# Value products in joint batches, unbroken first products of the compression, and another block order in the first feed-forward layer

## The chip, the cores and the metric

The kernel runs on one core of one Trainium2 chip. The metric is the device time of one execution in microseconds (us). Three runs of the kernel before took 1014.2, 1014.8 and 1014.85 us; their median is 1014.8 us.

## What is computed

The reference is a small transformer of two layers on one sequence of 256 tokens, 1024 wide, all in float32. Each layer is a feed-forward step, a mixer and a second feed-forward step, each added to the running `x`:

```python
x = x + 0.5 * swiglu(rms_norm(x, ffa_norm[l]), ffa_w_gate[l], ffa_w_up[l], ffa_w_down[l])
x = x + hybrid_mixer(rms_norm(x, mix_norm[l]), w_in[l], ...)
x = x + 0.5 * swiglu(rms_norm(x, ffb_norm[l]), ffb_w_gate[l], ffb_w_up[l], ffb_w_down[l])
```

`swiglu(x) = (silu(x @ w_gate) * (x @ w_up)) @ w_down`, with a hidden width of 2816. The mixer projects to 2840 columns. Eight of its heads (64 wide) do causal attention within the one block of 256 tokens. The other eight share two key-value heads and add three branches under sigmoid gates: attention over compressed blocks, over selected blocks, and within a window. At this length the selected blocks and the window each cover all earlier tokens, so that both are plain causal attention. The compression takes 32 tokens of 64 columns (2048 numbers) per block, multiplies by `w1` (2048 x 256), applies a gelu, and multiplies by `w2` (256 x 64). Both halves of the mixer are normalised and multiplied by `w_out`.

## The kernel before

Weights come as 1 MB transfers into five `raw` buffers. ScalarE rounds each half of such a buffer to float32r (`whi`, L301), VectorE takes the rest (`wlo`, L280), and TensorE adds three products, hi x hi, lo x hi and hi x lo (`prod3`, L320 to L322). There are six buffers for each of `whi` and `wlo`; TensorE frees them.

**Feed-forward.** Gate and up are cut into column blocks of 512. A plan, one per feed-forward step, is a list of tokens: `g0`, `u0`, `g2` ... are whole products of a gate or up block with all of `x` (48 matmuls of 512 columns each), `h5` is the last, half-wide block of both. For blocks 1 and 3, gate and up together are made from seven block products instead of eight (`product`): a token such as `63` is product 6 of block 3, 12 matmuls. These products need sums of weight blocks. A sum is made in place: product 1 is a plain load, and 5, 6 and 4 each add one more block to the same `raw` buffer with an accumulating transfer from GpSimd's queue (L260), once the split of the sum before has been read out of it; 3 and 7 share a second buffer in the same way. Plain loads go through SyncE's queue (L246, L237). The plan's order is at once the order of the products on TensorE, of the splits on ScalarE and VectorE, of the plain loads, and of the accumulating transfers. `rest` recombines the seven results on VectorE: L628 and L630 after product 6, L633 after product 7 (it reads the bank into which product 4 then adds), L638 to L653 for the gated halves. For a plain block, L573 multiplies gate by up (tile `sg`), and `turn` (L548) transposes the result on TensorE.

**Mixer.** After the scores and the exponentials, `apply` scales four 128 x 128 pieces of probabilities, transposes them (L1059), copies them into one of two `pT` tiles, and multiplies each by a 64-wide slice of values (L1077). These four value products are one batch. Each of them uses 64 of the array's columns, so the profile shows them as `128*64`; two neighbours lie in different halves. The first products of the compression (`hidden`, L1237) use 32 columns each, `128*32`; they are given out in four groups of four, with a pause between the groups in which other work may be put. A mixer has 18 batches and two sets of 16 compression products.

**What sets the order.** Every engine runs its own list of instructions, written when the program is built. `Flow` keeps an estimated clock for each engine and steps a set of generators; a `yield` names the estimated time, event or buffer that a generator waits for, and the one that is due first writes its next instructions. Estimated times order the instructions; the chip waits on semaphores.

Of the kernel before, what the change touches and what calls it, by code (L numbers as in the profile page):

```python
# [33 lines left out]
RB = 0  # L34
RA = 1
BAL = 0.4
TH0 = 2.0
COLD = 5.0
WARM = 8
ARRIVE = [4.4, 5.2, 6.7, 7.4], [8.9, 9.6, 11.1, 11.8]  # L40
ARRIVE_X = [3.5, 5.9, 8.1, 10.3]
HOP = 0.3
PLANS = ("g0 u0 g2 11 u2 51 21 31 g4 61 71 13 u4 41 53 23 33 h5 63 73 43".split(),) + (
    "g0 u0 11 g2 51 21 31 u2 61 71 13 g4 41 53 23 33 u4 63 73 h5 43".split(),) * 3
AC = 0.1
DV = 0.06
# [85 lines left out]
def hybrid_kernel(ctx, tc, x_in, ffa_norm, ffa_w_gate, ffa_w_up, ffa_w_down, mix_norm, w_in,  # L132
# [3 lines left out]
    nc = tc.nc  # L136
# [10 lines left out]
    fl = Flow()  # L147
    NRAW, NW, NP = 5, 6, 5
    for tag, n in (("acc", 4), ("sb", 2), ("tb", 2), ("raw", NRAW), ("w", NW),
                   ("work", 7), ("p", NP), ("pT", 2), ("pair", 1)):  # L150
        fl.pool(tag, range(n))

    def bank(tag, bufs):
# [660 lines left out]
    def mixer(l, us, nm, nxt):  # L814
# [6 lines left out]
        def carve(w, *shape):  # L821
            n = 1
            for s in shape:
                n *= s
            o = pos[w]
            pos[w] += n
            assert pos[w] <= 5632
            ap = (b1, b2)[w][:, o:o + n]
            names = "abcde"[:len(shape)]
            if len(shape) > 1:  # L830
                ap = ap.rearrange(f"p ({' '.join(names)}) -> p {' '.join(names)}",
                                  **{c: s for c, s in zip(names, shape)})
            return ap
# [13 lines left out]
        w2v = carve(1, 2, 64)  # L847
        posT = carve(1, 2, 16)
        kbd = carve(1, 2, 16)
        h1T = carve(1, 2, 32)  # L850
        hid = carve(1, 256)
        th = carve(1, 2, 32)
        gT = {k: gall[:, o + 4 * l:o + 4 * l + 4] for k, o in (("m", 48), ("n", 56))}
        cs = carve(1, T, 8, 16)
        pTs = [carve(w, 512) for w in range(2)]
        k1 = big.tile([128, 2, 512], F32R, name="k1", tag="nhi")
        k2 = big.tile([128, 2, 512], F32R, name="k2", tag="nlo")
        qs = [big.tile([128, 4, 256], F32R, name="qs", tag=z) for z in ("ohi", "olo")]
# [158 lines left out]
        class Group:  # L1017


            def __init__(self, left, close):  # L1020
                self.left, self.close, self.o = left, close, None
                self.asked, self.open = False, Event()
                self.begun = set()

        def apply(grp, e, t, ents, pp, sums, gate, late):

            n = 128 * (t + 1)
            yield e
            f = small.tile([128, 4], F32, name="f", tag="f", bufs=8)[:, :len(ents)]
            nc.vector.tensor_scalar(f, sums, 1e-30, None, op0=OP.max)  # L1030
            nc.vector.reciprocal(f, f)
            e = fl.on("dve", 0.42)
            if gate is not None:
                yield gate[0]
                fv = f.rearrange("p (b h) -> p b h", h=2) if len(ents) == 4 else f
                nc.vector.tensor_tensor(fv, fv, gate[1], OP.mult)
                e = fl.on("dve", 0.25)
            wait, e0 = [], e
            for i in range(len(ents)):
                p = pp[:, i * n:(i + 1) * n]  # L1040
                if fl.eng["act"] + 0.2 + BAL < fl.eng["dve"]:
                    wait.append(i)
                else:
                    nc.vector.tensor_scalar(p, p, f[:, i:i + 1], None, op0=OP.mult)
                    e = max(e, fl.dve(n // 2))
            if wait:
                yield e0
                for i in wait:
                    p = pp[:, i * n:(i + 1) * n]
                    nc.scalar.activation(p, p, AF.Copy, scale=f[:, i:i + 1])  # L1050
                    e = max(e, fl.act(n))
            yield e
            for k in late:
                yield event(*k)
            yield fl.get("tb")
            ps = tbank()
            todo = [(s_, i) for s_ in range(t + 1) for i in range(len(ents))]
            for j, (s_, i) in enumerate(todo):
                nc.tensor.transpose(ps[:, j * 128:(j + 1) * 128],  # L1059
                                    pp[:, i * n + s_ * 128:i * n + (s_ + 1) * 128], ident)  # L1060
            yield fl.pe(0.109 * len(todo))
            fl.put("p")
            pi = yield fl.get("pT")
            pT = pTs[pi]
            e = copy(pT, ps, 512)
            fl.put("tb", 0, e)
            yield e
            if not grp.asked:
                grp.asked = True
                yield fl.get("acc")  # L1070
                grp.o = bank("acc", 4)
                grp.open.set(fl.clock)
            yield grp.open
            for j, (s_, i) in enumerate(todo):
                h, val = ents[i]
                u = h % 2
                nc.tensor.matmul(grp.o[u * 64:(u + 1) * 64, h // 2 * 128:(h // 2 + 1) * 128], val(s_),  # L1077
                                 pT[:, j * 128:(j + 1) * 128], start=u not in grp.begun,
                                 stop=gate is None and s_ == t, skip_group_check=True)
                grp.begun.add(u)  # L1080
            e = fl.pe(0.135 * len(todo))
            fl.put("pT", pi, e)
            grp.left -= 1
            if grp.left == 0:
                fl.spawn(grp.close(grp, e))

        def tile_p(t, ents, scores, gate, late, grp, free):

# [138 lines left out]
        def hidden(b):  # L1227
            u = us[("w1k", "w1v")[b]]
            for r in u:
                yield r.landed[3]  # L1230
            yield event("blk", b)
            yield fl.get("acc")
            pc = bank("acc", 4)
            for j in range(4):
                for c in range(4):
                    i = c * 4 + j
                    nc.tensor.matmul(pc[c * 32:(c + 1) * 32, :256], blk[:, b, i].rearrange("p g n -> p (g n)"),  # L1237
                                     u[i // 8].tile.rearrange("p (j c) -> p j c", j=8)[:, i % 8],
                                     start=j == 0, stop=j == 3)
                fl.pe(0.5)  # L1240
                yield
            for r in u:
                fl.put("raw")
            fl.spawn(finish_cmp(b, pc))

        def finish_cmp(b, pc):
            yield fl.clock + HOP
            nc.scalar.activation(hid, pc[:, :256], AF.Copy)
            e = fl.act(256)
            fl.put("acc", 0, e)  # L1250
            yield e
            yield fl.get("tb")
            ps = tbank()
            for c in range(2):
                nc.tensor.matmul(ps[:, c * 32:(c + 1) * 32], hid[:, c * 128:(c + 1) * 128], tab["quad"],
                                 start=True, stop=True)
            yield fl.pe(0.3)
            hv = ps[:, :64].rearrange("p (c m) -> p c m", c=2)
            nc.scalar.activation(th, hv, AF.Square)
            yield fl.act(64)  # L1260
            nc.vector.scalar_tensor_tensor(th, th, 1.0 / GELU_K, hv, op0=OP.add, op1=OP.mult)
            yield fl.dve(64)
            nc.scalar.activation(th, th, AF.Tanh, scale=GELU_C * GELU_K)
            yield fl.act(64)
            po = ps[:, 128:192]
            if b == 0:
                nc.vector.scalar_tensor_tensor(h1T, th, 1.0, hv, op0=OP.add, op1=OP.mult)
                yield fl.dve(64)
                for c in range(2):
                    nc.tensor.matmul(po[:, :32], w2kd[:, c].rearrange("p u d -> p (u d)"), h1T[:, c],  # L1270
                                     start=c == 0, stop=c == 1)
                yield fl.pe(0.3)
                nc.vector.tensor_tensor(kbd, po[:, :32].rearrange("p (g n) -> p g n", g=2),
                                        tab["km"][:, :, None].to_broadcast([128, 2, 16]), OP.mult)
                e = fl.dve(32)
            else:
                nc.vector.scalar_tensor_tensor(th, th, 1.0, hv, op0=OP.add, op1=OP.mult)
                fl.dve(64)
                nc.vector.tensor_copy(hrep.rearrange("p c (r m) -> p c r m", r=4),
                                      th[:, :, None, :].to_broadcast([128, 2, 4, 32]))  # L1280
                yield fl.dve(256)
                for c in range(2):
                    nc.tensor.matmul(po, hrep[:, c], w2v[:, c], start=c == 0, stop=c == 1)
                yield fl.pe(0.4)
                nc.vector.tensor_tensor(vbd, po[:, None, :].to_broadcast([128, 8, 64]),
                                        tab["vm"].rearrange("p g r -> p (g r)")[:, :, None].to_broadcast([128, 8, 64]),
                                        OP.mult)
                e = fl.dve(512)
            fl.put("tb", 0, e)
            event("cmp", b).set(e)  # L1290

        def cmp_heads(t):
# [322 lines left out]
```

## Time and profile before

| what | value |
|---|---|
| median of three runs | 1014.8 us |
| the profiled execution: its own time | 1014.25 us |
| the profiled execution: its span, first to last instruction | 1012.5 us |
| TensorE matmuls busy | 994.3 us, 98% |
| VectorE busy | 739.1 us, 73% |
| ScalarE busy | 604.1 us, 60% |
| mean granted TensorE clock | 0.995 |

The profile is one execution. Busy times of engines overlap. TensorE's matmuls are pipelined: the length of a row is the time that one is under way, and rows overlap; the pace is the distance between their starts. "Granted clock" is the share of full speed that TensorE gets. The chain that ended last starts from the last instruction and goes back, at each step to what released it; its lengths add up without overlap.

### The profile page before, as it was taken

How to read it: one execution, taken by the hardware profiler on the slowest of the kernel's cores; microseconds unless marked ns; L12 is line 12 of the kernel's file. 1: busy time of each engine (PE TensorE's matmuls, PEld its weight loads, DVE VectorE, ACT ScalarE, POOL GpSimd, SP SyncE). 2: the span in 40 equal slices, each digit the busy share in tenths (PEclk: the TensorE clock that was granted, in tenths of full speed). 3: DMA queues.
4: the chain of work that ended last, by engine and by line, in shares of the span. 5: the costliest groups of instructions: out<-in, count | busy, mean ns of one | idle time of the engine just before them, and what ended most of it. 6: DMA issues, size and time to landing. Idle time of an engine off the chain costs nothing.

```text
span 1012.5 us, 14210 instructions
## 1 busy us (share of the span) xinstructions
PE 994.3 (98%) x5270; PEld 826.1 (82%) x5270; DVE 739.1 (73%) x1383; ACT 604.1 (60%) x1041; POOL 53.5 (5%) x61
## 2 busy tenths in 40 slices
PE   9999989999999999999999999999999999999996
PEld 7888768899877888888888888888978778888885
DVE  6988574588787978784488778447888789688544
ACT  7666543559666766653367566336695766665431
POOL 1011100100000011100001110001000001110000
PEclk9999989999999999999999999999999999999999
DMA  9999966363833599975649998553645238999611
GB/s 336 280 242 265 249 209 207 96 208 92 309 103 122 155 245 303 252 282 177 207 132 227 288 274 265 198 177 115 208 167 209 84 125 218 281 260 303 235 55 41
DMA packets 100981, 207.62 MB, mean 205 GB/s; under 512 B 3784, under 2 KB 23376, under 8 KB 100912
## 3 DMA queue, kind: packets, MB, share of 16 engines
q1 hardware_dynamic: 83072, 171.65, 48.9%
q0 software_dynamic: 17536, 34.54, 19.2%
q8 instruction: 41, 0.67, 0.3%
q10 hardware_dynamic: 304, 0.53, 0.1%
q14 instruction: 28, 0.23, 0.1%
HBM read 205.66 MB, written 1.05 MB: 204 GB/s over the span
## 4 chain that ended last, share of the span: by engine, by line
PE 90%; DMA 4%; DVE 3%; ACT 2%; issue 1%; DVEq 0%; POOL 0%; ACTq 0%; POOLq 0%
PE acc L320 18%; PE acc L321 18%; PE acc L322 18%; PE sb L322 6%; PE sb L320 6%; PE sb L321 6%; DMA raw<-in_ffb_w_up_dram 3%; PE acc L337 2%; PE acc L338 2%; PE acc L339 2%; PE acc L1077 2%; PE tb L548 2%; PE tb L1059 2%; DVE wlo L280 1%; DMA raw<-in_ffa_w_gate_dram 1%
## 5 line engine op out<-in xcount | busy, mean ns | idle before, releaser
L280 DVE TENSOR_TENSOR wlo<-raw,whi 128x1024 fp32r<-128x1024 f32 (+2 forms) x404 | 450.2, 1136 | 173.5 <-ACT whi L301 172.6
L301 ACT ACTIVATE whi<-raw 128x1024 fp32r<-128x1024 f32 (+2 forms) x404 | 388.7, 990 | 254.2 <-PE acc L322 107.4
L320 PE MATMUL acc<-whi,xhi 128*128 128x512 f32 (+1 forms) x336 | 133.1, 396 | 5.7 <-DVE p L633 5.7
L320 PE MATMUL acc<-whi,hhi 128*128 128x512 f32 x352 | 138.4, 393 | 0.0
L322 PE MATMUL acc<-whi,hlo 128*128 128x512 f32 x352 | 137.2, 390 | 0.0
L321 PE MATMUL acc<-wlo,hhi 128*128 128x512 f32 x352 | 137.0, 389 | 0.0
L321 PE MATMUL acc<-wlo,xhi 128*128 128x512 f32 (+1 forms) x336 | 128.9, 383 | 0.0
L322 PE MATMUL acc<-whi,xlo 128*128 128x512 f32 (+1 forms) x336 | 128.5, 382 | 0.0
L320 PE MATMUL sb<-whi,xhi 128*128 128x512 f32 x304 | 119.2, 392 | 0.0
L322 PE MATMUL sb<-whi,xlo 128*128 128x512 f32 x304 | 118.4, 390 | 0.0
L321 PE MATMUL sb<-wlo,xhi 128*128 128x512 f32 x304 | 118.3, 389 | 0.0
L320 PEld LDWEIGHTS acc<-whi,xhi 128*128 128x128 f32 x336 | 63.7, 189 | 17.2 <-ACT whi L301 6.1
L322 PEld LDWEIGHTS acc<-whi,hlo 128*128 128x128 f32 x352 | 66.1, 188 | 14.0
L321 PEld LDWEIGHTS acc<-wlo,hhi 128*128 128x128 f32 x352 | 66.1, 188 | 13.5
L320 PEld LDWEIGHTS acc<-whi,hhi 128*128 128x128 f32 x352 | 66.1, 188 | 13.2
L322 PEld LDWEIGHTS acc<-whi,xlo 128*128 128x128 f32 x336 | 63.6, 189 | 12.3
L321 PEld LDWEIGHTS acc<-wlo,xhi 128*128 128x128 f32 x336 | 63.7, 190 | 10.7 <-DVE wlo L280 0.2
L322 PEld LDWEIGHTS sb<-whi,xlo 128*128 128x128 f32 x304 | 57.0, 188 | 12.0
L321 PEld LDWEIGHTS sb<-wlo,xhi 128*128 128x128 f32 x304 | 57.1, 188 | 11.7
L320 PEld LDWEIGHTS sb<-whi,xhi 128*128 128x128 f32 x304 | 57.1, 188 | 11.6
L337 PE MATMUL acc<-xhi,whi 128*128 128x256 f32 x192 | 56.4, 294 | 0.0
L338 PE MATMUL acc<-xlo,whi 128*128 128x256 f32 x192 | 54.2, 282 | 0.0
(221 smaller groups left out, 1425.3 us busy)
## 6 DMA issues: line engine op xcount, KB each, us to landing
raw<-in_ffa_w_down_dram SPq DMA_DIRECT2D x22, 1024.0 KB, 5.1
raw<-in_ffb_w_down_dram SPq DMA_DIRECT2D x22, 1024.0 KB, 5.0
raw<-in_w_in_dram SPq DMA_DIRECT2D x20, 1024.0 KB, 5.1
raw<-in_ffb_w_gate_dram SPq DMA_DIRECT2D x20, 1024.0 KB, 5.3
raw<-in_ffa_w_gate_dram SPq DMA_DIRECT2D x18, 1024.0 KB, 7.5
raw<-in_ffa_w_up_dram SPq DMA_DIRECT2D x16, 1024.0 KB, 6.9
raw<-in_ffb_w_up_dram SPq DMA_DIRECT2D x16, 1024.0 KB, 7.0
raw<-in_ffa_w_up_dram POOLq DMA_DIRECT2D x12, 1024.0 KB, 9.1
```

The costliest lines, as they stand in the source:

```text
L280: nc.vector.tensor_tensor(view(u, lo, i, True), source(u, i), view(u, hi.bitcast(F32), i, True), OP.subtract)
L301: nc.scalar.activation(view(u, u.halves[-1][0], i, True), source(u, i), AF.Copy)
L320: nc.tensor.matmul(ps, xh, wh, start=first, stop=False, skip_group_check=True)
L321: nc.tensor.matmul(ps, xh, wl, start=False, stop=False, skip_group_check=True)
L322: nc.tensor.matmul(ps, xl, wh, start=False, stop=last, skip_group_check=True)
L337: nc.tensor.matmul(ps, wh, xs[0][:, k], start=first and j == 0, stop=False, skip_group_check=True)
L338: nc.tensor.matmul(ps, wh, xs[1][:, k], start=False, stop=False, skip_group_check=True)
L339: nc.tensor.matmul(ps, wl, xs[0][:, k], start=False, stop=last, skip_group_check=True)
L548: nc.tensor.transpose(ps[:, j * 128:(j + 1) * 128], h[:, j * 128:(j + 1) * 128], ident)
L1059: nc.tensor.transpose(ps[:, j * 128:(j + 1) * 128], pp[:, i * n + s_ * 128:i * n + (s_ + 1) * 128], ident)
L1077: nc.tensor.matmul(grp.o[u * 64:(u + 1) * 64, h // 2 * 128:(h // 2 + 1) * 128], val(s_), pT[:, j * 128:(j + 1) * 128], start=u not in grp. ...
```

## The change

Three parts. First, the tokens of the first feed-forward step stand in another order: `13` moves from behind `71` to ahead of `61`, `g4` from ahead of `61` to behind `71`, `u4` to behind `33`, and `h5` to behind `73`. Second, a batch of value products is put aside when its probabilities are ready; the next batch that comes gives out both, and a batch without a partner goes alone after an estimated 4 us. There are four `pT` tiles instead of two, and the planner's cost of a batch is changed. Third, the pause between the four groups of compression products is gone, so 16 of them follow each other; three small tiles of the compression move to the `work` buffers, where the added `pT` tiles take their place.

```diff
-PLANS = ("g0 u0 g2 11 u2 51 21 31 g4 61 71 13 u4 41 53 23 33 h5 63 73 43".split(),) + (
+PLANS = ("g0 u0 g2 11 u2 51 21 31 13 61 71 g4 41 53 23 33 u4 63 73 h5 43".split(),) + (
...
-                   ("work", 7), ("p", NP), ("pT", 2), ("pair", 1)):
+                   ("work", 7), ("p", NP), ("pT", 4), ("pair", 1)):
...
-        pTs = [carve(w, 512) for w in range(2)]
+        pTs = [carve(i % 2, 512) for i in range(4)]
...
-            for j, (s_, i) in enumerate(todo):
...
-            e = fl.pe(0.135 * len(todo))
-            fl.put("pT", pi, e)
...
+            def values():
+                for j, (s_, i) in enumerate(todo):
...
+                e = fl.pe(0.08 * len(todo))
+                fl.put("pT", pi, e)
+                grp.left -= 1
+                if grp.left == 0:
+                    fl.spawn(grp.close(grp, e))
...
+            ready.append(values)
+            if len(ready) < 2:
+                yield fl.clock + PARTNER
+            if values in ready:
+                while ready:
+                    ready.pop(0)()
+                fl.pe(0.3)
...
                                      start=j == 0, stop=j == 3)
                 fl.pe(0.5)
-                yield
...
+            yield fl.get("work")
+            room = wk([128, 512], "cmp")
+            hid = room[:, :256]
+            th, h1T = (room[:, o:o + 64].rearrange("p (c m) -> p c m", c=2) for o in (256, 320))
```

**TensorE, first mixer, in the middle of the attention.** `acc<-m` are value products (one row of x4 is a batch), `sb<-k,qs` scores, `tb<-ident,p` transposes of probabilities, `acc<-raw,m` compression products. Before:

```order
L1077 MATMUL acc<-m_1641 64x128 x4
L1117 MATMUL sb<-k_1643,qs 128x512
L1118 MATMUL sb<-k_1644,qs 128x512
L1117 MATMUL sb<-k_1643,qs 128x512
L1118 MATMUL sb<-k_1644,qs 128x512
L1077 MATMUL acc<-m_1642,m_1641 64x128 x4
L1059 MATMUL tb<-ident,p 128x128 x4
L1237 MATMUL acc<-raw,m_1641 32x256 x16
L1077 MATMUL acc<-m_1641 64x128 x4
L1237 MATMUL acc<-raw,m_1641 32x256 x4
```

and now, about the same place (line numbers are 1 to 15 higher from here on):

```order
L1079 MATMUL acc<-m_1641 64x128 x4
L1079 MATMUL acc<-m_1642,m_1641 64x128 x4
L1128 MATMUL sb<-k_1643,qs 128x512
L1129 MATMUL sb<-k_1644,qs 128x512
L1128 MATMUL sb<-k_1643,qs 128x512
L1129 MATMUL sb<-k_1644,qs 128x512
L1059 MATMUL tb<-ident,p 128x128 x4
L1248 MATMUL acc<-raw,m_1641 32x256 x16
L1059 MATMUL tb<-ident,p 128x128 x4
L1248 MATMUL acc<-raw,m_1641 32x256 x16
```

Two batches stand together that stood apart, and the compression's 16 products are one row each time, with one row of transposes between the two sets. Over the rows of a whole mixer, value batches stood in 15 places and now stand in 10. The number of places at which the used part of the array changes between one matmul and the next (128*128, 128*64, 128*32, 64*128) goes from 80 to 60 in the two mixers together.

**SyncE's queue, first feed-forward step: the plain loads of gate and up blocks.** The rows begin behind the loads of `21` and `31`. Before:

```order
L246 DMA raw<-in_ffa_w_gate_dram 128x4x512 x3
L246 DMA raw<-in_ffa_w_up_dram 128x4x512 x2
L246 DMA raw<-in_ffa_w_gate_dram 128x4x512
L246 DMA raw<-in_ffa_w_up_dram 128x4x512
L237 DMA raw<-in_ffa_w_gate_dram 128x4x256
L237 DMA raw<-in_ffa_w_up_dram 128x4x256
L237 DMA raw<-in_ffa_w_gate_dram 128x4x256
L237 DMA raw<-in_ffa_w_up_dram 128x4x256
```

and now:

```order
L247 DMA raw<-in_ffa_w_gate_dram 128x4x512 x4
L247 DMA raw<-in_ffa_w_up_dram 128x4x512 x3
L238 DMA raw<-in_ffa_w_gate_dram 128x4x256
L238 DMA raw<-in_ffa_w_up_dram 128x4x256
L238 DMA raw<-in_ffa_w_gate_dram 128x4x256
L238 DMA raw<-in_ffa_w_up_dram 128x4x256
```

The load of `13` now comes first, the two of `g4` behind it, then those of `23`, `33` and `u4`, and the four half-size ones of `h5` last; before, `13` stood third and `u4` ahead of `23`. The order of the eight accumulating transfers on GpSimd's queue (`51 61 71 41 53 63 73 43`) is as before.

**VectorE, first feed-forward step, where the last products of block 3 are prepared.** `raw_585` before, and `raw_480` and `raw_788` now, are buffers that hold sums of block 3: before, the two rows of `raw_585` are the last sum, that of `43`. Before:

```order
L583 SCALAR_TENSOR_TENSOR sg_1125<-sb_1053,rs_100,sg_1125 128x256
L583 SCALAR_TENSOR_TENSOR sg_1131<-sb_1061,rs_100,sg_1131 128x256
L280 TENSOR_TENSOR wlo_1145<-raw_585,whi_1144 128x1024
L628 TENSOR_TENSOR p_853<-p_853,acc_1127 128x512
L630 TENSOR_TENSOR p_1005<-p_1005,p_853 128x512
L555 TENSOR_TENSOR hlo_122<-tb_1140,hhi_121 128x2x128
L280 TENSOR_TENSOR wlo_1156<-raw_585,whi_1155 128x1024
L555 TENSOR_TENSOR hlo_122<-tb_1151,hhi_121 128x2x128
L633 TENSOR_TENSOR p_1005<-acc_1158,p_1005 128x512
```

and now, where `raw_480` is the sum of `63`, `raw_788` that of `73`, and `raw_901` the first load of `h5`; `sg_864` and `sg_873` are gate times up of block 4:

```order
L281 TENSOR_TENSOR wlo_973<-raw_480,whi_972 128x1024
L281 TENSOR_TENSOR wlo_984<-raw_480,whi_983 128x1024
L281 TENSOR_TENSOR wlo_999<-raw_788,whi_998 128x1024
L281 TENSOR_TENSOR wlo_1010<-raw_788,whi_1009 128x1024
L281 TENSOR_TENSOR wlo_1026<-raw_901,whi_1025 128x1024
L574 SCALAR_TENSOR_TENSOR sg_864<-sb_967,rs_100,sg_864 128x512
L574 SCALAR_TENSOR_TENSOR sg_873<-sb_975,rs_100,sg_873 128x512
L281 TENSOR_TENSOR wlo_1045<-raw_901,whi_1044 128x1024
L556 TENSOR_TENSOR hlo_122<-tb_1055,hhi_121 128x4x128
```

Before, the first half of `43`'s split stood ahead of the three sums of which the last lets product `43` begin. Now both halves of `73`'s split and one of `h5` stand ahead of block 4's gated result, which TensorE transposes in the middle of product `63`.

## Rows read from the trace of the kernel before

**Rows 1.** Stretches: length; PE, PEld, DVE, ACT, POOL busy; PEclk, DMA share, GB/s.

```profile
12.00:32.00 20.00, 20.00 (x89) 16.23 (x88) 16.47 (x32) 16.00 (x25) 0.00 (x0) 1.00 1.05 386
37.00:125.00 88.00, 88.00 (x403) 72.85 (x402) 68.35 (x93) 52.18 (x63) 11.21 (x12) 1.00 0.97 251
125.00:128.00 3.00, 0.40 (x2) 0.00 (x0) 1.96 (x3) 3.00 (x5) 0.00 (x0) 1.00 0.01 3
128.00:131.00 3.00, 0.00 (x0) 0.00 (x0) 3.00 (x6) 3.00 (x4) 0.00 (x0) 0.51 0.00 0
200.00:330.00 130.00, 128.97 (x959) 109.00 (x958) 106.39 (x353) 91.69 (x247) 1.23 (x3) 1.00 0.50 164
```

**Rows 2.** Chain that ended last, 100 to 160 us: start, length, what.

```profile
111.78 13.06 DMA raw<-in_ffa_w_gate_dram
124.92 1.07 ACT whi L301
126.01 1.22 DVE wlo L280
130.36 0.61 DVE p L633
131.10 0.76 PE acc L320
...
135.16 0.23 PE acc L320
```

**Rows 3.** DMA issues from 59, 109, 111.5 us; last column: us to landing.

```profile
raw<-in_ffa_w_up_dram POOLq DMA_DIRECT2D x1, 1024.0 KB, 9.1
raw<-in_ffa_w_down_dram SPq DMA_DIRECT2D x1, 1024.0 KB, 9.3
raw<-in_ffa_w_gate_dram POOLq DMA_DIRECT2D x1, 1024.0 KB, 13.1
```

**Rows 4.** Issues on GpSimd and SyncE, by time: start, length, what, [idle before].

```profile
59.53 1.29 POOL L260 DMA_DIRECT2D raw<-in_ffa_w_up_dram  x1 [6.04 <-DVE p L758]
...
109.24 0.37 SPq L246 DMA_DIRECT2D raw<-in_ffa_w_down_dram  x1
```

**Rows 5.** TensorE around 66, 77 and 79 us: start, length, what.

```profile
65.75 0.39 PE L320 MATMUL sb<-whi,xhi 128*128 128x512 f32 x1
76.63 0.39 PE L320 MATMUL acc<-whi,fnhi 128*128 128x512 f32 x1
79.35 0.39 PE L320 MATMUL acc<-whi,fohi 128*128 128x512 f32 x1
```

**Rows 6.** TensorE, first mixer, one batch of value products alone.

```profile
250.23 0.28 PE L339 MATMUL acc<-xhi,wlo 128*128 128x256 f32 x1
250.44 0.66 PE L1077 MATMUL acc<-m 128*64 128x128 f32 x8
251.02 0.50 PE L1117 MATMUL sb<-k,qs 128*128 128x512 f32 x1
251.36 0.40 PE L1118 MATMUL sb<-k,qs 128*128 128x512 f32 x1
```

**Rows 7.** TensorE, first mixer, two batches of value products in succession.

```profile
242.58 0.40 PE L1118 MATMUL sb<-k,qs 128*128 128x512 f32 x1
242.91 0.66 PE L1077 MATMUL acc<-m 128*64 128x128 f32 x8
243.40 0.61 PE L1077 MATMUL acc<-m,m 128*64 128x128 f32 x8
243.94 1.09 PE L1059 MATMUL tb<-ident,p 128*128 128x128 f32 x8
...
244.99 0.28 PE L338 MATMUL acc<-xlo,whi 128*128 128x256 f32 x1
245.10 0.28 PE L339 MATMUL acc<-xhi,wlo 128*128 128x256 f32 x1
```

**Rows 8.** Chain that ended last, first mixer: eight transposes.

```profile
239.75 0.87 PE tb L1059 x8
```

More of the change, by code (lines that the diff above doesn't have):

```diff
@@ L36 @@
 BAL = 0.4
+PARTNER = 4.0
 TH0 = 2.0
@@ L849, in mixer @@
         kbd = carve(1, 2, 16)
-        h1T = carve(1, 2, 32)
-        hid = carve(1, 256)
-        th = carve(1, 2, 32)
         gT = {k: gall[:, o + 4 * l:o + 4 * l + 4] for k, o in (("m", 48), ("n", 56))}
         cs = carve(1, T, 8, 16)
-        pTs = [carve(w, 512) for w in range(2)]
+        pTs = [carve(i % 2, 512) for i in range(4)]
         k1 = big.tile([128, 2, 512], F32R, name="k1", tag="nhi")
@@ L1023, in __init__ @@
                 self.begun = set()
+        ready = []
         def apply(grp, e, t, ents, pp, sums, gate, late):
@@ L1073, in apply @@
             yield grp.open
-            for j, (s_, i) in enumerate(todo):
[L1075 to L1080, printed above, removed]
-            e = fl.pe(0.135 * len(todo))
-            fl.put("pT", pi, e)
-            grp.left -= 1
-            if grp.left == 0:
-                fl.spawn(grp.close(grp, e))
+            def values():
+                for j, (s_, i) in enumerate(todo):
+                    h, val = ents[i]
+                    u = h % 2
+                    nc.tensor.matmul(grp.o[u * 64:(u + 1) * 64, h // 2 * 128:(h // 2 + 1) * 128], val(s_),
+                                     pT[:, j * 128:(j + 1) * 128], start=u not in grp.begun,
+                                     stop=gate is None and s_ == t, skip_group_check=True)
+                    grp.begun.add(u)
+                e = fl.pe(0.08 * len(todo))
[10 more added lines that the diff above has]
+                fl.pe(0.3)
         def tile_p(t, ents, scores, gate, late, grp, free):
@@ L1289, in finish_cmp @@
             fl.put("tb", 0, e)
+            fl.put("work", 0, e)
             event("cmp", b).set(e)
```

## The prediction

> **What bounds the kernel now.** I read the table of busy times first: TensorE is busy for 98% of the span, so a change counts only where it shortens TensorE's own work or one of its few waits. The windows by stage come next, and they show two quite different stretches [rows 1]. In the first feed-forward step (37 to 125 us) TensorE is busy for all 88 us while the DMA engines are busy for 0.97 of the time: two limits are nearly equal. Right behind it TensorE stands still: 0.40 us of work from 125 to 128, none from 128 to 131, with a granted clock of 0.51, the lower of its two levels. In the first mixer (200 to 330 us) TensorE works 128.97 of 130 us, and the DMA share is 0.50; there the length is the sum of TensorE's work and nothing else.
>
> The chain of waits tells what the stall was [rows 2]. The transfer that adds the last block to the sum of product 43 is issued at 111.78 and takes 13.06 us, to 124.84. Then come the rounding on ScalarE (1.07), the rest on VectorE (1.22), and VectorE's queue up to the sum on L633, which ends at 130.97 and lets product 43 start at 131.10. TensorE's idle time released by L633 is 5.7 us in the page's group of L320. The 4.06 us from 131.10 to 135.16 hold nine matmuls that the full clock would pass in 9 x 0.23 = 2.07, so the fallen clock cost another 2.0. The stall costs 7.7 us in all.
>
> **Mixers: what joining a batch is worth.** The matmuls are the same in number and shape; what changes is where the used part of the array changes between neighbours. The profile keeps two records for each product, so that x8 is one batch of four. A batch alone stands between a 256-wide matmul at 250.23 and a 512-wide one, whose successor starts at 251.36 [rows 6]. From these 1.13 us I take one 256-wide pace (0.12) and one 512-wide pace (0.23): the batch and its two borders cost 0.78. Two batches in succession go from 242.58 to the 256-wide pair's first row at 244.99 [rows 7]. Of these 2.41 us, 0.23 are a 512-wide matmul, 0.87 is the row of transposes x8 (its length in the chain, [rows 8]) and 0.12 a 256-wide pace: two batches cost 1.19, where two alone would cost 1.56. Joining saves 0.37, which takes away two changes of the array's used part; that is 0.19 a change. From the other side: at the transposes' pace, 0.87 / 8 = 0.109, the eight products of rows 7 take 0.87 and leave 0.32 for two borders, 0.16 each; the four of rows 6 take 0.44 and leave 0.34, 0.17 each. I take 0.17. The order of the rows has 80 such changes in both mixers together before and 60 now: 20 x 0.17 = 3.4 us saved, between 3.2 and 3.9; and nothing, if what is saved in rows 7 belongs to the transposes beside them.
>
> What the change adds there: a batch may wait for its partner, an estimated 4 us by the plan, and the compression now needs a `work` buffer before its gelu. Behind such a wait the generator only gives nothing out; TensorE is filled with projections and scores, as the 1.0 us of idle time in 130 shows [rows 1]. I cost both at nothing. If that cover were gone once, at the end of each mixer, the two waits would cost up to 8 us; nothing excludes a small loss either. The row nearest to it is the 1.0 us of idle time, so I take zero. The planner's changed figures only move instructions, which the count of changes has in it.
>
> **First feed-forward step: what is late next.** With `h5` behind `73`, product 43 has 10.88 us more work in front of it. That is how long a whole product takes, from 65.75 to 76.63; a block product takes 2.72, from 76.63 to 79.35 [rows 5]. So 43's sum is no longer the late one. What now has least in front of it is 73's sum: VectorE splits both its halves, and one of `h5`, ahead of block 4's gated result, and TensorE transposes that result in the middle of product 63.
>
> When does 73's sum land? GpSimd's transfer for 71 is issued at 59.53 and takes 9.1: 68.6 [rows 3, 4]. From there I step through the transfers in the order in which they can be asked for, the DMA engines being full. For the step of an accumulating transfer I take the last one seen: SyncE's load issued at 109.24 lands 9.3 later, at 118.5 [rows 3, 4], and 43's sum lands at 124.84, which is 6.3 behind it. A plain 1 MB load steps 1.05 MB / 386 GB/s = 2.7 us [rows 1]. The accumulation for 41 gives 74.9, for 53 81.2; the loads of 23, 33 and two halves of u4 (4 x 2.7) 92.0; 63's accumulation 98.3; h5's first load 101.0; 73's accumulation 107.3. Then 0.1 to start, the rounding 1.07, three splits on VectorE (3 x 1.22) and the gated product, for which I take the like-sized 0.61 of L633 [rows 2]: 107.3 + 5.4 = 112.7. That is when the transposes of block 4 can begin.
>
> When does TensorE get there? The same products up to 65.75, then seven block products (13 61 71 41 53 23 33: 19.04), two whole ones (g4, u4: 21.76), half of 63 (1.36) and two groups of transposes x4 at half of 0.87 each: 108.8. It waits 112.7 - 108.8 = 3.9 us, small waits before it included, since they fall into the same gap. Behind it stand half of 63, 73 and h5, some 15 us, before 43 is due at about 128; 43's sum, one step of 6.3 later than 73's, lands near 113.6 and has 14 us in hand, so the old stall goes altogether. Nothing downstream gives the gain back: the later stages are bound by TensorE's sum. The step gains 7.7 - 3.9 = 3.8.
>
> **The sum.** -3.4 - 3.8 = -7.2 us on the profiled execution's own 1014.25 gives 1007.05; the median of the three runs stands 0.55 above that execution, so I forecast 1007.6 and, since a lower gain in the mixers is the more likely error, write 1007.9.
>
> **Rivals.**
> *The clock falls again.* The old gap of 5.7 us ended at the lower level [rows 1, 2]. A gap of 3.9 is shorter, and the rows show no other long one. If it falls as before, 2.0 us more: 1009.9.
>
> *The accumulating transfers don't queue behind the loads.* If 63's and 73's step in with the loads in turn, each lands one load (2.7 us) earlier at least: 73 by 104.6, the gap at most 1.2 us, time 1005.2. For it: the first accumulation above took 9.1 us to land although loads were queued. Against it: 43's was issued 2.5 us behind a load and landed 6.3 behind it [rows 3, 4], as if it had stood at the end of the line.
> The Trainium skill, "DMA: Bandwidth & Descriptors", section "Queues, rings and completion order", says that each DMA engine takes the queues with work in turn, a packet at a time, so that GpSimd's transfer would share the engines with SyncE's loads and not stand behind all of them. By that rule the time would be this rival's; 43's 13.1 us against 71's 9.1 disagrees with it so far.
>
> *Nothing from joining.* If the cost sits with each batch and not with the borders, the 3.4 goes: 1011.3.
>
> *Slower: 73's sum is later still.* Sums of block 3 are made in place, each waiting for the split of the one before to be read out. If 63's and 73's transfers each take 13.1 us as 43's did, and not 71's 9.1 [rows 3], 73 lands 8 later, at 115.3; TensorE stands for 11.9 us, its clock falls (2.0), and the step costs 13.9 in place of 7.7: 1007.9 + 8 + 2 = 1017.9. This gets slower than before by over 0.2% (2.0 us, about what a measurement here can tell from no change) once 73 lands later than about 114.
>
> *The joining doesn't happen or waits uncovered*, and the feed-forward gains what rows 2 promise: between 1011 and 1015, within the 0.2%.
>
> **Chances.** Forecast 0.45 (own range 1005.8 to 1009.5), fallen clock 0.22, transfers in turn 0.17, nothing from joining 0.05, later sum 0.06, covered by nothing 0.05. The range from 1003.8 to 1012.3 takes in the first four, the clock case and the no-joining one with some room, and leaves out the slow rival, half of the last, and a gain over 11 us. Faster by over 0.2%: 0.45 + 0.22 + 0.17 + 0.05, less a little for a mis-sized sum: 0.88. Within 0.2%: 0.06. Slower: 0.06.
>
> **What would show it.** No idle time before product 43 and none at the lower clock from 125 to 131; in its place one gap of 3 to 4 us near 109 to 113, at the transposes of `turn`, released by VectorE's `sg`; 73's accumulating transfer landing near 107; the granted clock in that gap's window tells the first rival. In the mixers, pairs of batches as one row x16 of about 1.2 us, and from the projections to the first `w_out` row some 1.7 us less in each of the two. I am wrong if TensorE waits for a partner or a `work` buffer in the mixers, if the gap stands before another product of block 3 than 63, or if 73 lands after 110 or before 104.

## The result

The changed kernel takes 1003.42 us (median of 4 runs, 1003.0 to 1004.15), the kernel before 1014.5 beside it: a ratio of 0.989, 95% interval 0.9879 to 0.9902. That is 11.1 us less. The prediction was 1007.9 with a range from 1003.8 to 1012.3: right in sign, too small, and the time lies 0.4 us below the range. A second set of runs gave 1003.95 against 1014.85 (0.9888, 0.9872 to 0.9905).

The changed kernel's windows, to be laid beside [rows 1] (length; PE, PEld, DVE, ACT, POOL busy; PEclk, DMA share, GB/s):

```profile
37.00:125.00 88.00, 87.08 (x394) 70.84 (x393) 74.99 (x100) 55.45 (x66) 11.21 (x12) 1.00 0.97 255
125.00:128.00 3.00, 3.00 (x15) 2.47 (x14) 2.10 (x4) 1.55 (x3) 0.00 (x0) 1.00 1.02 418
128.00:131.00 3.00, 3.00 (x16) 2.45 (x15) 2.22 (x4) 2.72 (x5) 0.00 (x0) 1.00 0.55 223
200.00:330.00 130.00, 129.05 (x971) 111.67 (x970) 106.40 (x350) 95.29 (x253) 0.00 (x0) 1.00 0.48 160
```

The two windows in which TensorE did 0.40 us of work are now full and at the full clock. In return, 0.9 us of idle time stands between 37 and 125 us. TensorE's list of waits over the whole span (us in total, times, longest) names it in its last two rows; the two waits of the first row stand in the mixers, as in the kernel before:

```profile
PE acc L322 <- DVE wlo L281: 1.6, 2, 0.8
...
PE sb L322 <- DVE wlo L281: 0.6, 1, 0.6
PE tb L549 <- DVE z L644: 0.3, 1, 0.3
```

(The two left out stand before 8 us, where the kernel starts.) The 5.7 us released by L633 is gone; so is a wait of 0.4 us (two of 0.2) for the compressed attention's value products, L1337 in the kernel before. The gap of 3.9 us that the prediction put at the transposes of block 4 (L549 from `sg`) is not in the list at all.

Where the gain lies is read from the first `w_down` product of each feed-forward step. First the kernel before with only the new token order (`plan_only`, a run of the next section), then the changed kernel, then the first such row of the kernel before:

```profile
131.28 0.39 PE L320 MATMUL acc<-whi,hhi 128*128 128x512 f32 x1
444.33 0.40 PE L320 MATMUL acc<-whi,hhi 128*128 128x512 f32 x1
625.52 0.40 PE L320 MATMUL acc<-whi,hhi 128*128 128x512 f32 x1
938.53 0.40 PE L320 MATMUL acc<-whi,hhi 128*128 128x512 f32 x1
```

```profile
130.76 0.39 PE L321 MATMUL acc<-whi,hhi 128*128 128x512 f32 x1
441.21 0.40 PE L321 MATMUL acc<-whi,hhi 128*128 128x512 f32 x1
622.40 0.40 PE L321 MATMUL acc<-whi,hhi 128*128 128x512 f32 x1
933.03 0.40 PE L321 MATMUL acc<-whi,hhi 128*128 128x512 f32 x1
```

```profile
136.05 0.48 PE L320 MATMUL acc<-whi,hhi 128*128 128x512 f32 x1
```

From the first row to the second, and from the third to the fourth, lies one mixer each with the work around it, a mixer stage: 313.05 and 313.01 with the old mixers, 310.45 and 310.63 with the new. The mixers gave 2.6 and 2.4, together 5.0 us; forecast was 3.4. In the kernel before, the first of these products starts at 136.05, so the first feed-forward step gave 5.3 us; forecast was 3.8. The two parts account for 10.3 of the 10.7 us between the profiled spans (1012.5 and 1001.8); the kernel before's profiled execution also lost some 0.5 in its second mixer's stage (313.55), which `plan_only` with the same mixers does not show.

### The profile page after: what moved, and what is told of

Same layout as the page of the kernel before. It is cut to its first block, busy times and chain, and to the rows that moved or that the text cites. A ratio compares the mean times of both kernels' runs of the same rounds, so it can differ in the third digit from the quotient of the medians.

```text
span 1001.8 us, 14198 instructions
## 1 busy us (share of the span) xinstructions
PE 988.3 (99%) x5270; PEld 825.7 (82%) x5270; DVE 735.8 (73%) x1369; ACT 608.0 (61%) x1055; POOL 53.5 (5%) x61
## 4 chain that ended last, share of the span: by engine, by line
PE 86%; DMA 4%; DVE 2%; ACT 1%; issue 1%; DVEq 0%; POOL 0%; ACTq 0%
PE acc L321 17%; PE acc L322 17%; PE acc L323 17%; PE sb L323 6%; PE sb L321 6%; PE sb L322 6%; PE acc L338 2%; DMA raw<-in_ffa_w_up_dram 2%; PE acc L339 2%; PE acc L340 2%; PE acc L1079 2%; PE tb L1059 2%; DMA raw<-in_ffa_w_gate_dram 2%; PE tb L549 2%; PE tb L407 1%; DVE wlo L281 1%
## 5 line engine op out<-in xcount | busy, mean ns | idle before, releaser
L322 PE MATMUL acc<-wlo,hhi 128*128 128x512 f32 x352 | 137.0, 389 | 0.0
L322 PE MATMUL acc<-wlo,xhi 128*128 128x512 f32 (+1 forms) x336 | 128.1, 381 | 0.0
L322 PE MATMUL sb<-wlo,xhi 128*128 128x512 f32 x304 | 118.4, 390 | 0.6 <-DVE wlo L281 0.6
L322 PEld LDWEIGHTS acc<-wlo,hhi 128*128 128x128 f32 x352 | 66.1, 188 | 13.3
L322 PEld LDWEIGHTS acc<-wlo,xhi 128*128 128x128 f32 x336 | 63.2, 188 | 10.7 <-DVE wlo L281 0.2
L322 PEld LDWEIGHTS sb<-wlo,xhi 128*128 128x128 f32 x304 | 57.1, 188 | 12.6 <-DVE wlo L281 1.0
L340 PE MATMUL acc<-xhi,wlo 128*128 128x256 f32 x192 | 54.2, 282 | 0.0
```

What stands on the lines that cost most here:

```text
L322: nc.tensor.matmul(ps, xh, wl, start=False, stop=False, skip_group_check=True)
L340: nc.tensor.matmul(ps, wl, xs[0][:, k], start=False, stop=last, skip_group_check=True)
```

## The experiments

**The parts one by one.** `plan_only` is the kernel before with the new line of PLANS; `mix_only` is the changed kernel with the old one.

```diff
-PLANS = ("g0 u0 g2 11 u2 51 21 31 g4 61 71 13 u4 41 53 23 33 h5 63 73 43".split(),) + (
+PLANS = ("g0 u0 g2 11 u2 51 21 31 13 61 71 g4 41 53 23 33 u4 63 73 h5 43".split(),) + (
```

> The kernel before with only the new token order of the first feed-forward step. Theory A (the parts act separately; the feed-forward step is worth what its stage shows, first w_down matmul 5.3 us earlier): 5 to 5.6 us below the kernel before, first w_down matmul near 130.8, no gap before product 43, both mixers as long as before (their shares of TensorE's wait at the compressed attention's value products, 0.38 us each, still there). Rival B (the plan gave only the 3.8 us of the prediction, and the rest of the gain came from the mixers): 3.5 to 4 us. Rival C (the new order also shifts the mixers' loads): 6.5 us or more.

> The changed kernel with the old token order in the first feed-forward step: only the mixers' changes. Theory A: 5.0 to 5.6 us below the kernel before, 2.4 in the first mixer and 2.9 in the second; the stall of 5.7 us before product 43 is back, with the lower clock behind it. Rival B: 6.5 us or more below, if the feed-forward gave only what was predicted. Rival C: 3.4 us below, the 20 changes of the array's used part at 0.17 and nothing else.

Measured: 1009.12 against 1014.33 (0.9946, 0.9934 to 0.9959) and 1008.91 (0.9949, 0.9936 to 0.9961), that is 5.2 and 5.4 us. The sum, 10.6, is the whole change within the intervals: the parts act separately, as theory A has it, and both terms of the prediction's sum were too small. In `mix_only` the wait for the last sum is back (first row), in `plan_only` the wait of 0.2 us before the compressed attention's products stays (second row):

```profile
PE acc L321 <- DVE p L634: 5.0, 1, 5.0
```

```profile
PE acc L1337 <- ACT m L307: 0.4, 2, 0.2
```

**Which part of the mixers' change.** `no_join` gives out every batch at once; `broken` puts the pause between the compression's groups back; `unbroken_only` gives out every batch at once and also takes the planner's old cost of a batch, so that of the mixers' change only the unbroken products (and the tiles) remain.

```diff
 # no_join
-            if len(ready) < 2:
+            if len(ready) < 1:
 # broken
                 fl.pe(0.5)
+                yield
 # unbroken_only: no_join, and
-                e = fl.pe(0.08 * len(todo))
+                e = fl.pe(0.135 * len(todo))
...
-                fl.pe(0.3)
```

> The changed kernel in which every batch of value products goes out alone, at once; compression's products stay unbroken. The program has 82 changes of the array's used part against 66 in the changed kernel and 86 in the kernel before. Theory A (0.17 to 0.18 us a change): 2.7 to 2.9 us slower than the changed kernel, and the wait before the compressed attention's value products stays away. Rival D (joining itself is worth nothing, the shorter compression is what counts): within 0.7 us of the changed kernel. Rival E (joining also takes away waits): 4 us or more slower.

> The changed kernel with the pause between the four groups of compression products put back, joining kept; 64 changes of the array's used part. Theory A (the unbroken products finish the compression some 3 us sooner and so take away the wait of 0.38 us before the compressed attention's value products in each mixer): that wait is back, 0.4 to 0.8 us slower than the changed kernel, less 0.35 for two changes fewer. Rival D (the compression is where the mixers' extra gain of 1.9 us over the forecast came from): 1.9 us slower. Rival F: no difference, within 0.3 us.

> The new token order and the unbroken compression products; every batch of value products goes out alone with the planner's old cost of a batch, four pT tiles stay. 82 changes of the array's used part (86 in the kernel before, 66 in the changed kernel). Theory A (0.18 us a change; the waits of the run without joining came from the planner's changed costs, not from the lack of joining): 4 x 0.18 = 0.7 us below the kernel with the new token order alone, so near 1008.4, with the wait of 0.38 before the compressed attention's value products still there in both mixers. Rival E (batches alone beside unbroken products bring their own waits): near 1012, as without joining.

`broken`: 1003.5 us (0.9896, 0.9882 to 0.9909), no different from the changed kernel: rival F. The wait before the compressed attention's products is not back; TensorE's waits between 190 and 450 us that this run lists are

```profile
PE tb L407 <- DVE x L1431: 0.2, 1, 0.2
```

so theory A's step, that the unbroken products take that wait away, falls. The two waits of 0.8 us in the mixers are not listed either, and yet the two mixer stages are only 0.2 and 0.3 us shorter than the changed kernel's (310.27 and 310.29): a wait that leaves the list is not its whole length gained. `unbroken_only`: 1009.49 us (0.9943, 0.9931 to 0.9956), against 0.9946 for the new token order alone, so the unbroken products by themselves are worth nothing that these runs can tell; the 0.7 expected was not found. Its mixer stages, 312.85 and 313.25, say the same beside `plan_only`'s 313.05 and 313.01. Its waits in the same stretch are the old ones:

```profile
PE acc L322 <- DVE wlo L281: 0.8, 1, 0.8
PE acc L1351 <- ACT m L308: 0.2, 1, 0.2
```

It is joining together with its planner costs, then, that brings the mixers' gain: by these the changed kernel differs from `unbroken_only`, and the ratios are 0.989 and 0.9943. No run separates the two; `no_join` shows that planner costs alone can move the time by some 3 us.

`no_join` was the miss of this group: 1012.2 us (0.9979, 0.997 to 0.9988), 8.8 us above the changed kernel, where theory A said 2.7 to 2.9 and rival E 4 or more. It has two waits in each mixer that no other run has at that length, and in the second mixer TensorE's clock fell behind them (windows; columns as above):

```profile
PE acc L322 <- DVE wlo L281: 1.8, 1, 1.8
PE acc L1352 <- ACT m L308: 1.1, 1, 1.1
```

```profile
809.00:812.00 3.00, 1.09 (x4) 0.49 (x3) 2.76 (x11) 0.35 (x1) 0.00 (x0) 1.00 0.00 0
812.00:816.00 4.00, 4.00 (x12) 3.20 (x13) 2.88 (x3) 0.00 (x0) 0.00 (x0) 0.67 0.72 219
```

From `unbroken_only` it differs in the planner's cost of a batch alone (0.32 + 0.3 us instead of 0.54). 0.08 us of estimate per batch moved instructions (468 of the 5270 places in TensorE's order hold another instruction) so that some 3 us more were lost: 2.7 by the two medians, 3.3 by each one's distance from the kernel before beside it. The prediction had said that these figures "only move instructions", and counted nothing for that beyond the changes.

**What decides in the first feed-forward step.** `h5_first` and `h5_between` move only `h5`:

```diff
-... 33 u4 63 73 h5 43
+... 33 u4 h5 63 73 43      # h5_first
+... 33 u4 63 h5 73 43      # h5_between
```

> The changed kernel with h5 ahead of 63 instead of behind 73 (... 33 u4 h5 63 73 43). Theory G (what decides in block 3 is how many splits stand ahead of block 4's gated result on VectorE, and how much product work stands ahead of 43): all of h5's splits now stand ahead of the gated result, so TensorE waits 4 to 6 us at the transposes of block 4 near 107 us, and 1.5 to 2.5 us more before product 43, which again has only 73 in front of it: 6 to 9 us slower than the changed kernel. Rival I (only the landing of the sums counts, and h5 in front of 63 covers all of them): within 1 us of the changed kernel.

> The changed kernel with h5 between 63 and 73 (... u4 63 h5 73 43). Theory G: the transposes of block 4 wait no longer than in the changed kernel (under 0.6 us), and product 43, with only 73 in front of it, waits for the three sums of which L634 is the last: 1 to 2 us slower than the changed kernel. Rival I: within 0.5 us of the changed kernel, 43's sum being covered by h5 and 73 together.

`h5_first`: 1013.65 us (0.9984, 0.9975 to 0.9993), 9.7 us above the changed kernel's 1003.95 of the later runs. That is more than the 6 to 9 of theory G, but both waits came as it has them, 4.4 us at block 4's transposes and 1.8 before product 43, and the clock fell behind both. The first wait, and the two windows behind it:

```profile
PE tb L549 <- DVE sg L574: 4.4, 1, 4.4
```

```profile
113.00:116.00 3.00, 2.19 (x8) 1.80 (x8) 2.96 (x5) 0.60 (x1) 0.16 (x1) 0.50 0.96 345
116.00:120.00 4.00, 4.00 (x14) 3.33 (x13) 0.97 (x2) 0.60 (x1) 1.12 (x1) 0.54 0.56 103
```

`h5_between`: 1011.48 us (0.9966, 0.9952 to 0.9979), 7.5 us above the changed kernel where 1 to 2 were expected. The wait before product 43 came as expected (1.4 us, for L634's sum), but the transposes waited too, 4.5 us instead of under 0.6: theory G had this run wrong. Its waits from 104 to 116 us show why:

```profile
ACT whi L302 <- DMA raw<-in_ffa_w_up_dram: 9.6, 2, 5.3
DVE wlo L281 <- ACT whi L302: 8.9, 2, 4.9
...
PE tb L549 <- DVE sg L574: 4.5, 1, 4.5
```

VectorE was not busy with splits; it stood, because the last split ahead of the gated result was now one of `h5`'s second buffer, for whose load ScalarE waited until 111.98:

```profile
111.98 2.00 ACT L302 ACTIVATE whi<-raw 128x1024 fp32r<-128x1024 f32 x2 [4.29 <-DMA raw<-in_ffa_w_up_dram]
```

In `h5_first` it was the splits: five of them stand ahead of the gated result, two from 106.65 on and then, 0.6 us behind them, these three:

```profile
109.59 3.50 DVE L281 TENSOR_TENSOR wlo<-raw,whi 128x1024 fp32r<-128x1024 f32 x3 [0.58 <-ACT whi L302]
```

So not only the number of splits counts, but also which landing the last of them waits for. That mends theory G, and it is the same mechanism as in the prediction's sum.

**A version with fewer changes of the array's used part.** `join4` lets up to four batches go together; `join4_order` also changes tokens.

```diff
-PARTNER = 4.0
+PARTNER = 5.0
...
-            if len(ready) < 2:
+            if len(ready) < 4:
 # join4_order, in PLANS
-... 13 61 71 g4 41 53 ...
+... 13 61 g4 71 53 41 ...
```

> The changed kernel in which up to four batches of value products go out together and a batch waits an estimated 5 us for partners instead of 4. 58 changes of the array's used part against 66. Theory A: 8 x 0.18 = 1.4 us below the changed kernel from the changes, and 0.8 us more if TensorE's wait of 0.8 us in each mixer's out products is as short as in the run with the broken compression: near 1001. Rival H (a longer wait for partners is uncovered): a wait of 1 us or more at the value products or the out products in each mixer, and not below the changed kernel.

> The changed kernel once more, beside the two runs below, so that they are compared on the same chip. Every theory: 10.5 to 11.5 us below the kernel before, and the 0.5 us by which the second mixer gained more than the first in the first comparison should not be seen between this profile and the earlier one of the changed kernel (it lay in the profiled execution of the kernel before).

> Up to four batches together, an estimated 5 us of waiting for partners, once more. Theory A: 1.0 to 2.0 us below the changed kernel of the same call. Rival: within 0.5 us of it, the first difference being one between chips.

> Up to four batches together, and the tokens g4 71 53 41 in place of 71 g4 41 53, so that a whole product stands ahead of 71, whose split and sums made g4 wait for its second operand (0.6 to 0.75 us near 75 us). Theory J (that wait was for VectorE's queue behind 71's sum): the wait near 75 us is gone, and 0.3 to 0.8 us come off the kernel without this order. Rival K (53 ahead of 41 or the later landing of 73's sum brings a gap at the transposes of block 4, some 2 us): 1 us or more slower than without this order.

`join4` took 1002.3 and, beside the changed kernel's 1003.95, 1001.93 us; `join4_order` 1002.33. The ratios to the kernel before are 0.9873 (0.9859 to 0.9886), 0.988 (0.9862 to 0.9897) and 0.9872 (0.9858 to 0.9887), the changed kernel's 0.989 and 0.9888. All three lie lower, but the intervals overlap. In both its profiles the span is 1000.3 or 1000.4 us, in the changed kernel's two 1001.8 and 1002.8; the two waits of 0.8 us in the mixers are no longer listed. The mixer stages are 309.5 and 310.2 in the first profile, 309.4 and 310.2 in the second, against 310.5 and 310.6 or 310.7. So `join4` is likely an improvement, by 1 to 2 us. In `join4_order` the wait near 75 us is gone as theory J has it, and two others stand in its place, so nothing is gained:

```profile
90.09 0.63 PE L549 MATMUL tb<-ident,z 128*128 128x128 f32 x4 [0.64 <-DVE z L644]
...
121.72 0.52 PE L549 MATMUL tb<-ident,z 128*128 128x128 f32 x3 [0.94 <-DVE z L644]
```

`changed_again` repeated the changed kernel's two mixer stages within 0.1 us (310.5 and 310.7).

## Why the prediction was wrong, point by point

**The bound and the stall: right.** Product 43 no longer waits, the lower clock behind it is gone, and nothing downstream gives the gain back. The rivals of a fallen clock and of a later sum did not happen. One term in this was wrong without harm: 43's sum landed at 118.6, not at 113.6 (issued at 102.35, 16.2 us to landing), and the step of 6.3 has no term for the three loads issued between 73's transfer and 43's. The margin of 14 us hid it.

**The new gap: right in place, mis-sized.** Its four rows in the changed kernel, on ScalarE, VectorE and TensorE:

```profile
105.39 2.01 ACT L302 ACTIVATE whi<-raw 128x1024 fp32r<-128x1024 f32 x2 [4.78 <-DMA raw<-in_ffa_w_up_dram]
```

```profile
106.48 3.50 DVE L281 TENSOR_TENSOR wlo<-raw,whi 128x1024 fp32r<-128x1024 f32 x3 [4.43 <-ACT whi L302]
109.90 1.40 DVE L574 SCALAR_TENSOR_TENSOR sg<-sb,rs,sg 128x512 f32<-128x512 f32 x2
```

```profile
110.32 0.39 PE L323 MATMUL acc<-whi,fnlo 128*128 128x512 f32 x1
110.70 1.31 PE L549 MATMUL tb<-ident,sg 128*128 128x128 f32 x8
```

Every step of the chain is there: three splits, the gated product, the transposes. From landing to transposes I had 5.4 us; 105.3 to 110.70 is 5.4. What failed is the term before it, the landing of 73's sum. I let it land at 107.3, with a whole `h5` load of 2.7 us and an accumulating step of 6.3 behind 63's 98.3. 63's landed at 98.49 (predicted 98.3; 41's at 75.05, predicted 74.9), but 73's came 6.8 later, not 9.0. The issues of that time, with KB and us to landing, for `h5`'s first pair (issued at 89.48 and 89.90) and for 73's (at 93.11):

```profile
raw<-in_ffa_w_gate_dram SPq DMA_DIRECT2D x1, 512.0 KB, 10.9
raw<-in_ffa_w_up_dram SPq DMA_DIRECT2D x1, 512.0 KB, 15.8
```

```profile
raw<-in_ffa_w_up_dram POOLq DMA_DIRECT2D x1, 1024.0 KB, 12.2
```

The load I had counted as 1 MB is 512 KB, as the order's `128x4x256` says; by its size alone the estimate is 98.5 + 1.35 + 6.3 = 106.1. For the other 0.8 the rows speak for the rival of transfers served in turn, which said 104.6 at the latest and was half right: 73's accumulation, issued 3.2 us after `h5`'s second load, landed some 0.4 us before it (93.11 + 12.2 = 105.3, and 89.90 + 15.8 = 105.7). On the other side TensorE came later than my 108.8, at 110.55 (the last row above and one pace of 0.23): two rows show how.

```profile
74.45 0.39 PE L321 MATMUL sb<-whi,xhi 128*128 128x512 f32 x1
75.43 0.50 PE L322 MATMUL sb<-wlo,xhi 128*128 128x512 f32 x1 [0.59 <-DVE wlo L281]
```

From 74.45 to 75.43 is 0.98 for one pace of 0.23: `g4` waits 0.75 us for its second operand, and 0.23 more at the transposes inside it (79.19 to 79.65). The first products came 0.5 us later in this execution (8.05 in place of 7.55), which is luck of the execution and not of the change. These make 1.5 of the 1.75. So the sum was there almost when TensorE was: the pause before the transposes at 110.70 is 0.15 us. With 0.42 at the transposes at 121.83, the gap of 3.9 shrank to small waits of 1.6 in all, in places for which the prediction had only said that they "fall into the same gap". 7.7 less 1.6 and less the late start of 0.5 is 5.6; the stage shows 5.3, and the rest is not accounted for.

**The mixers: the price was right or a little low, the sum incomplete.** Two batches that came joined, in the changed kernel; [rows 7] answer to them:

```profile
237.47 0.40 PE L1129 MATMUL sb<-k,qs 128*128 128x512 f32 x1
237.79 0.66 PE L1079 MATMUL acc<-m 128*64 128x128 f32 x8
238.28 0.61 PE L1079 MATMUL acc<-m,m 128*64 128x128 f32 x8
238.82 1.09 PE L1059 MATMUL tb<-ident,p 128*128 128x128 f32 x8
239.67 0.37 PE L338 MATMUL acc<-xhi,whi 128*128 128x256 f32 x1
```

A 512-wide matmul takes 0.32 instead of 0.23 ahead of a change, and two batches go by in 1.03. What lies above the usual pace at the changes, summed over the starts of all TensorE matmuls of a mixer stage, depends on how much behind a change is counted with it. With the last matmul ahead of each change and the first three behind it, it is 6.7 us in `plan_only` (41 changes; the order's rows gave 40) and 5.0 in the changed kernel (31, where they gave 30): 0.16 a change, and 3.4 saved in both mixers. But 64-wide products start in pairs and 32-wide ones in fours; counted so that no such group is cut (two behind a change, four where 32-wide products begin), it is 8.3 and 6.05: 0.20 a change, and 4.5 saved. So the changes brought 3.4 to 4.5 of the 5.0 us, against the 3.4 forecast, and what else there is was not in the sum. 0.76 us is one wait, here in the kernel before (first fence) and at the same product now:

```profile
279.35 0.27 PE L1327 MATMUL tb<-ident,m 128*128 128x128 f32 x1
...
280.15 0.40 PE L322 MATMUL acc<-whi,xlo 128*128 128x512 f32 x1
280.76 0.38 PE L1337 MATMUL acc<-m 128*128 128x128 f32 x1 [0.21 <-ACT m L307]
```

```profile
272.62 0.33 PE L1342 MATMUL tb<-ident,m 128*128 128x128 f32 x1
...
273.24 0.40 PE L323 MATMUL acc<-whi,xlo 128*128 128x512 f32 x1
273.57 1.16 PE L1185 MATMUL sb<-m 64*128 64x128 f32 x16
274.66 1.16 PE L1352 MATMUL acc<-m 128*128 128x128 f32 x8
```

From 280.15 to 280.76 is 0.61 for a pace of 0.23: 0.38 a mixer, in which TensorE waited for ScalarE's copy of the transposed probabilities. Now a row of sixteen scores stands in between and covers it. With joining it went (`broken`, the changed kernel), without it stayed (`unbroken_only`, `plan_only`). Some 0.6 more is spread over 512-wide matmuls that stand a few ns closer; why stays open, and since the second count, this wait and the 0.6 together come to more than 5.0, the shares are not settled. The unbroken compression brings four of the twenty changes; by the price that would be 0.7 us, and alone it did not change the time.

**The range.** It was built around one mechanism per part, most with the miss on the side of loss. The case that the new gap nearly closes was there with 0.17 and gave 1005.2, but nothing was allowed above 3.9 us for the mixers, and the two gains together were not a case.

## What to carry to other kernels

When a chain of transfers decides, take each one's size from the row or the tile that is moved, and take the arrival of the other side with all its small waits: a gap is the difference of two sums, and here the one came 2.0 us earlier and the other 1.75 later, so that both errors closed the gap. When instructions are put together, price the borders, but ask also which known small wait the new neighbours cover; the list of waits before the change had it. A planner's cost figure is an edit of the order: 0.08 us in an estimate was worth some 3 us on the chip.

## What the runs showed of the hardware that was not expected

Two loads of 512 KB issued 0.42 us apart took 10.9 and 15.8 us to land, and an accumulating transfer of 1 MB from GpSimd's queue, issued behind both, landed between them. From 93.0 to 93.5 us the profile has 41 packets of GpSimd's queue and 25 of SyncE's, so the two shared the engines then; the time to landing of such a load says little about its size. And the same wait of 1.77 us before L322 occurred in both mixers of `no_join`; behind the first the granted clock stayed at 1.00 (315 to 319 us), behind the second it was 0.67 (812 to 816 us). In `h5_first` a wait of 1.8 us before product 43 was followed by the lower clock (0.84 from 134 to 138 us). A gap of that length does not settle what the clock does; behind the waits of 4.4 and 4.5 us it fell both times (0.50 in `h5_first`, 0.64 in `h5_between`, from 113 to 116 us):

```profile
315.00:319.00 4.00, 2.53 (x11) 2.13 (x12) 3.97 (x6) 0.00 (x0) 0.00 (x0) 1.00 0.35 74
```

```profile
134.00:138.00 4.00, 2.17 (x8) 1.44 (x7) 4.00 (x7) 1.29 (x2) 0.00 (x0) 0.84 0.73 235
```

The first fence is `no_join`, the second `h5_first`.
